# Second mixer of a two-layer decoder trunk: second pair's rotations and splits traced at high priority, compressed weights built amid the token branches, fewer scaling steps

## The chip, the cores and the metric

The kernel runs on one core of a Trainium2 chip. The metric is device time in microseconds (us), from the start to the end of one execution; 3 runs of the kernel before gave 672.49 to 674.24 us, with a median of 673.55 us. The engines that matter here are PE (matrix multiply, with transposes done as a multiply by the identity), DVE (elementwise and reductions), ACT (activations, copies out of PSUM), and SP, whose queue issues the weight loads.

## The reference, cut to what matters

A sequence of 256 tokens with 1024 features goes through two layers. Layer 0 has two attention mixers side by side, layer 1 has one mixer with three branches; behind each stands a SwiGLU FFN. The change lies in the mixer of layer 1:

```
q = rope(q).reshape(B, T, 4 groups, 4 heads, 64)
k_cmp, v_cmp = compress(rope(kc_raw), ...), compress(vc_raw, ...)   # 15 blocks of 32 tokens
p_cmp = safe_softmax(q . k_cmp * scale, block already ended)
o_cmp = p_cmp . v_cmp
o_slc = softmax(q . k_slc * scale, causal) . v_slc     # selected blocks
o_win = softmax(q . k_win * scale, causal, 512 back) . v_win
out   = g0 * o_cmp + g1 * o_slc + g2 * o_win           # g = sigmoid gates, per head
x     = x + out @ w_out
```

With 256 tokens there are 4 blocks of 64 and the 16 best are kept, so that every block is selected; the window of 512 covers all tokens. Both token branches are therefore plain causal softmaxes, over different keys and values.

## The kernel before, in words

**Precision.** A product with weights is made of three PE passes: a weight tile is split by ACT into `w_hi` (L108) and by DVE into `w_lo`, the rest (L109), activations likewise, and hi.hi, hi.lo and lo.hi are summed (`mm3`, L270 to L272). Each of the 2 x 128 tokens is a row tile, t = 0 and t = 1.

**The mixer of layer 1** (`odd_mixer`). Its 16 heads are worked in two pairs of groups, gp = 0 ("first pair") and gp = 1 ("second pair"), 8 heads each. For each pair:
- `project` makes q for both row tiles in PSUM (tile `ps_in`, 512 wide, eight 128-feature steps); `rope` on DVE rotates it (L318, L320 twice, L323) into `nq`; ACT and DVE split it into `stk` (L214, L215); PE transposes it (`pt_q`, L751) and ACT writes it out as `qS`.
- a second `project` gives the keys of both token branches (`nk`, rotated and split the same way, transposed as `pt_k`, then written by ACT as `kS` and, with its halves swapped, `kX`) and the values `vv`.
- the compressed branch, for each t: eight small matmuls into `ps_c`, and on DVE a softmax over 16 blocks for eight heads at once (L788 to L798), which ends in a transpose `pt_c` and a copy `cT`.
- the token branches, for each t and for even and odd heads (`par`): matmuls into `ps_s` (L822), then per head and branch a masked row minimum on DVE (L327) and an exponential with its sum on ACT (L328); on DVE the reciprocal of the sums (L831), their product with the gates (L832), and one scaling per head and branch (L836); then PE transposes the weights (`pt_p`, L841), ACT copies them to `pT`.
- for each t the output `ps_o`: compressed values (L849) and then token values (L857) summed in one PSUM tile; ACT and DVE split it into `aT` (L214, L215).

Then `residual` multiplies `aT` by the output weights (`ps_out`, L270 to L272), adds it to x (L308), and the next norm makes `xg` (L234) and transposes it (`pt_a`) for the FFN, whose first product is `ps_g`.

**What sets the order.** The program is traced in Python order; a scheduler in the compiler then orders each engine's instructions by priority (earlier traced first) and by when it thinks their operands and buffers are ready. Instructions passed to `pin` (`keep_in_program_order`) keep their order. Each engine runs its list strictly in order. Buffers come from pools with a fixed number of slots per tag: PSUM has 4 banks for `mm` (the projections and `ps_out`), 2 for `s` (`ps_s`, `ps_c`) and 2 for `tp` (all transposes and `ps_o`); `stk` has 2, `qS` has 3, `kS`, `kX`, `vv` and `pT` have 2, `sc` has 1 and `cT` has 2. So a later pair's transposes need the same two `tp` banks that the earlier pair's `pt_p` and `ps_o` use.

Of the kernel before, what the change touches and what calls it, by code (L numbers as in the profile page):

```python
# [10 lines left out]
AF = mybir.ActivationFunctionType  # L11
ALU = mybir.AluOpType
# [5 lines left out]
P = 128  # L18
NT = T // P
# [101 lines left out]
def trunk(tc, x, w0, w1, sm0, cw, vec, cst, out, dbg=None):  # L121
    nc = tc.nc
    V, A, G, TE = nc.vector, nc.scalar, nc.gpsimd, nc.tensor

    from contextlib import ExitStack
# [16 lines left out]
    def nat(name):  # L142
        return ap.tile([P, 512], F32, tag="nat", bufs=4, name=name)
# [25 lines left out]
    for h in range(2):  # L169
        c = slice(512 * h, 512 * h + 512)  # L170
# [18 lines left out]
    def evac(dst, src):  # L189
        A.activation(dst, src, AF.Copy)  # L190
# [83 lines left out]
    def project(aT, w):  # L274

        kk = 2
        n = KD // kk
        ps = [mm_bank("ps_in") for _ in range(NT)]
        for g in range(n):
            wh, wl = W.next()  # L280
            for i in range(kk):
                for t in range(NT):
                    mm3(ps[t][:, :w], aT[t], g * kk + i, wh[:, i], wl[:, i], g == 0 and i == 0, g == n - 1 and i == kk - 1)
        return ps
# [353 lines left out]
    def odd_mixer(nm, goff):  # L638
        aT, rs = nm.aT, nm.rs
        with tc.tile_pool(name="odd", bufs=1, reuse_waits="tile") as pool:  # L640
# [113 lines left out]
            for gp in range(2):  # L754
# [3 lines left out]
                vv = pool.tile([P, NT, 256], F32, tag="vv", bufs=2, name="vv")  # L758
                ps = project(aT, 512)
                for t in range(NT):  # L760
                    nq = nat("nq").rearrange("p (b d) -> p b d", d=64)
                    rope(pool, nq, ps[t].rearrange("p (b d) -> p b d", d=64), rs[t], t, 8, 64)
                    for h0 in (0, 4):
                        evac(qS[t][:, h0 : h0 + 4], stacked(nq[:, h0 : h0 + 4], 4, "pt_q"))
# [3 lines left out]
                for t in range(NT):  # L768
                    nk = nat("nk")[:, :256].rearrange("p (b d) -> p b d", d=64)
                    rope(pool, nk, ps[t][:, :256].rearrange("p (b d) -> p b d", d=64), rs[t], t, 4, 64)  # L770
                    A.activation(vv[:, t], ps[t][:, 256:], AF.Copy, scale=rs[t])
                    pt = stacked(nk, 4, "pt_k").rearrange("p (b r) c -> p r b c", b=2)
                    tq = slice(t * P, (t + 1) * P)
                    evac(kS[:, :, :, tq], pt)
                    for z in range(2):
                        evac(kX[64 * z : 64 * z + 64, :, :, tq], pt[64 * (1 - z) : 64 * (1 - z) + 64])


                cTs = []
                for t in range(NT):  # L780
# [22 lines left out]
                    cTs.append(cT)  # L803

                for t in range(NT):
# [5 lines left out]
                    for par in range(2):  # L811
                        pT = pool.tile([P, 2 * D], F32, tag="pT", bufs=2, name="pT")[:, : 2 * nst * 512].rearrange("p (b k j c) -> p b k j c", b=2, k=nst, j=4)
                        pTs.append(pT)
                        for j0 in range(0, 4, g):
# [14 lines left out]
                            cf = den[:, : 2 * g].rearrange("p (g b) -> p g b", b=2)  # L829
                            h0 = 2 * j0 + par  # L830
                            V.reciprocal(cf, cf)  # L831
                            V.tensor_mul(cf, cf, gates[t][:, gp, h0 : h0 + 2 * g - 1 : 2, 1:3])  # L832
                            for i in range(g):
                                for b in range(2):
                                    z = 2 * i + b
                                    V.tensor_scalar(e[:, i, b], e[:, i, b], den[:, z : z + 1], None, op0=ALU.mult)  # L836
# [11 lines left out]
                    for j in range(4):  # L848
                        mmi = TE.matmul(ob[:, j * P : (j + 1) * P], vbd[:, gp, 2 * j : 2 * j + 2].rearrange("p a d -> p (a d)"), cTs[t], start=j == 0, stop=False, skip_group_check=True)  # L849
                        if j:  # L850
                            pin(mmi)
# [152 lines left out]
```

## Time and profile before

| | |
|---|---|
| median of 3 runs | 673.55 us (672.49 to 674.24) |
| the profiled execution, its time | 673.14 us |
| its span, first to last instruction | 671.4 us |
| PE, DVE, ACT busy | 646.6, 492.2, 394.8 us |
| granted TensorE clock, mean | 0.997 |

The page's busy times are sums of instruction durations with overlaps removed. Matmuls are pipelined and their ends are modelled, so a PE that is shown busy can still be waiting a little between two starts: starts are the safer reading. The mixer of layer 1 spans about 340 to 479 us; the token branches of both pairs lie between 380 and 470 us.

### The profile page before, as it was taken

How to read it: one execution, taken by the hardware profiler on the slowest of the kernel's cores; microseconds unless marked ns; L12 is line 12 of the kernel's file. 1: busy time of each engine (PE TensorE's matmuls, PEld its weight loads, DVE VectorE, ACT ScalarE, POOL GpSimd, SP SyncE). 2: the span in 40 equal slices, each digit the busy share in tenths (PEclk: the TensorE clock that was granted, in tenths of full speed). 3: DMA queues.
4: the chain of work that ended last, by engine and by line, in shares of the span. 5: the costliest groups of instructions: out<-in, count | busy, mean ns of one | idle time of the engine just before them, and what ended most of it. 6: DMA issues, size and time to landing. Idle time of an engine off the chain costs nothing.

```text
span 671.4 us, 10018 instructions
## 1 busy us (share of the span) xinstructions
PE 646.6 (96%) x3505; PEld 537.5 (80%) x3505; DVE 492.2 (73%) x1132; ACT 394.8 (59%) x801; POOL 12.4 (2%) x24
## 2 busy tenths in 40 slices
PE   5999999999999999999999999969999999999995
PEld 4978788778888888888887877746788888888884
DVE  5999977669777787543588899696787777775424
ACT  5785748548555555433375688686675555554322
POOL 1000000000000000000000000000000000000000
PEclk9999999999999999999999999999999999999998
DMA  8844454138666666662295431400485555555601
GB/s 314 286 136 154 126 171 144 31 137 290 201 188 188 188 187 186 189 191 75 64 387 214 158 126 31 145 14 1 156 288 189 188 187 188 186 188 187 189 0 63
DMA packets 31874, 109.68 MB, mean 163 GB/s; under 512 B 3536, under 2 KB 3792, under 8 KB 31568
## 3 DMA queue, kind: packets, MB, share of 16 engines
q1 hardware_dynamic: 31392, 108.45, 49.8%
q8 instruction: 28, 0.46, 0.3%
q10 hardware_dynamic: 432, 0.59, 0.2%
q14 instruction: 22, 0.18, 0.1%
HBM read 107.98 MB, written 1.05 MB: 162 GB/s over the span
## 4 chain that ended last, share of the span: by engine, by line
PE 83%; DVE 6%; ACT 5%; DMA 3%; issue 2%; POOL 1%; SPq 0%; POOLq 0%; DVEq 0%; ACTq 0%
PE ps_g L365 12%; PE ps_u L365 12%; PE ps_out L272 7%; PE ps_out L271 7%; PE ps_out L270 7%; PE ps_u L366 6%; PE ps_g L366 6%; PE ps_in L270 4%; PE ps_in L271 4%; PE ps_in L272 4%; DMA w_raw<-in_w 3%; PE ps_o L857 2%; PE pt_p L841 2%; DVE w_lo L109 1%; ACT w_hi L108 1%
## 5 line engine op out<-in xcount | busy, mean ns | idle before, releaser
L109 DVE TENSOR_TENSOR w_lo<-w_raw,w_hi 128x1024 fp32r<-128x1024 f32 (+5 forms) x200 | 235.2, 1183 | 95.9 <-ACT w_hi L108 93.1
L108 ACT ACTIVATE w_hi<-w_raw 128x1024 fp32r<-128x1024 f32 (+5 forms) x200 | 203.2, 1023 | 142.2 <-PE ps_out L272 60.5
L365 PE MATMUL ps_g<-aW,w_hi 128*128 128x512 f32 x352 | 125.6, 399 | 0.0
L365 PE MATMUL ps_u<-aW,w_hi 128*128 128x512 f32 x352 | 125.5, 399 | 0.0
L366 PE MATMUL ps_u<-aW,w_lo 128*128 128x256 f32 x352 | 98.9, 281 | 0.0
L366 PE MATMUL ps_g<-aW,w_lo 128*128 128x256 f32 x352 | 98.9, 281 | 0.0
L365 PEld LDWEIGHTS ps_g<-aW,w_hi 128*128 128x128 f32 x352 | 66.1, 188 | 16.7 <-DVE aW L215 0.3
L365 PEld LDWEIGHTS ps_u<-aW,w_hi 128*128 128x128 f32 x352 | 66.2, 188 | 16.4
L270 PE MATMUL ps_in<-w_hi,aW 128*128 128x512 f32 (+5 forms) x208 | 77.5, 373 | 1.0 <-ACT aW L214 0.9
L272 PE MATMUL ps_in<-w_hi,aW 128*128 128x512 f32 (+5 forms) x208 | 77.0, 372 | 0.0
L271 PE MATMUL ps_in<-w_lo,aW 128*128 128x512 f32 (+5 forms) x208 | 76.6, 369 | 0.0
L272 PE MATMUL ps_out<-w_hi,hT_lo 128*128 128x512 f32 x176 | 69.4, 395 | 0.0
L271 PE MATMUL ps_out<-w_lo,hT_hi 128*128 128x512 f32 x176 | 69.1, 392 | 0.0
L270 PE MATMUL ps_out<-w_hi,hT_hi 128*128 128x512 f32 x176 | 68.4, 389 | 0.0
L366 PEld LDWEIGHTS ps_u<-aW,w_lo 128*128 128x128 f32 x352 | 66.5, 189 | 0.0
L366 PEld LDWEIGHTS ps_g<-aW,w_lo 128*128 128x128 f32 x352 | 66.5, 189 | 0.0
L270 PEld LDWEIGHTS ps_in<-w_hi,aW 128*128 128x128 f32 x208 | 39.8, 192 | 6.2 <-ACT aW L214 1.6
L328 ACT ACTIVATE e<-e,bias 128x128 f32<-128x128 f32 (+1 forms) x96 | 42.4, 446 | 3.1 <-DVE bias L327 3.1
L272 PEld LDWEIGHTS ps_in<-w_hi,aW 128*128 128x128 f32 x208 | 39.6, 191 | 4.6 <-DVE aW L215 0.5
L271 PEld LDWEIGHTS ps_in<-w_lo,aW 128*128 128x128 f32 x208 | 39.6, 191 | 4.4 <-issue 0.4
L271 PEld LDWEIGHTS ps_out<-w_lo,hT_hi 128*128 128x128 f32 x176 | 33.0, 188 | 7.6
L270 PEld LDWEIGHTS ps_out<-w_hi,hT_hi 128*128 128x128 f32 x176 | 33.0, 188 | 7.3
(215 smaller groups left out, 887.9 us busy)
## 6 DMA issues: line engine op xcount, KB each, us to landing
w_raw<-in_w SPq DMA_DIRECT2D x176, 512.0 KB, 4.3
w_raw<-in_w SPq DMA_DIRECT2D x8, 384.0 KB, 4.1
gain<-in_vec SPq DMA_DIRECT2D x4, 512.0 KB, 5.5
cw<-in_cw SPq DMA_DIRECT2D x2, 1024.0 KB, 7.4
w_raw<-in_w SPq DMA_DIRECT2D x4, 416.0 KB, 6.7
w_raw<-in_w SPq DMA_DIRECT2D x4, 328.0 KB, 6.4
w_raw<-in_w SPq DMA_DIRECT2D x4, 304.0 KB, 2.9
x<-in_x SPq DMA_DIRECT2D x4, 256.0 KB, 5.8
```

What stands on the lines that cost most here:

```text
L108: nc.scalar.activation(hi[:, :n], raw[:, :n], AF.Copy)
L109: nc.vector.tensor_sub(lo[:, :n], raw[:, :n], hi[:, :n])
L270: TE.matmul(ps, act[0][:, k], wh, start=start, stop=False)
L271: TE.matmul(ps, act[0][:, k], wl, start=False, stop=False)
L272: TE.matmul(ps, act[1][:, k], wh, start=False, stop=stop)
L328: A.activation(e, e, AF.Exp, scale=-1.0, bias=bias, accum_out=den)
L365: TE.matmul(dst[f], wh[:, i, c], wide[:, k].rearrange("p z q -> p (z q)"), start=k == 0, stop=False)
L366: TE.matmul(dst[f][:, :T], wl[:, i, c], wide[:, k, 0], start=False, stop=k == KD - 1)
L841: TE.transpose(pt[:, i, b, st], e[:, i, b, st * P : (st + 1) * P], ident)
L857: pin(TE.matmul(ob[64 * par : 64 * par + 64], vv[:, st, c : c + 64], pTs[par][:, b, st].rearrange("p j c -> p (j c)"), start=False, stop=l ...
```

## The change: what it does, and the diff

1. For the second pair only, the rotation of q and of the keys, their splits, transposes and copies are traced inside `tc.high_priority()`, which puts them ahead of everything else that is ready.
2. The compressed branch is no longer worked for t = 0 and t = 1 ahead of the token branches. `compressed(t)` is called inside the loop over t, between the even and the odd heads of that t.
3. Scaling. For t = 0 the four scalings of a group (128 columns each) become one product of 512 columns with the gated reciprocals spread out. For t = 1 the product of reciprocals and gates is dropped, and each scaling (256 columns) takes two per-row factors, the reciprocal and the gate.

```diff
+                def soon():
+                    return tc.high_priority() if gp else nullcontext()
                 ps = project(aT, 512)
-                for t in range(NT):
-                    nq = nat("nq")...
+                with soon():
+                    for t in range(NT):
+                        nq = nat("nq")...            # rope, stacked, evac as before
...
                 ps = project(aT, 512)
-                for t in range(NT):
-                    nk = nat("nk")...
+                with soon():
+                    for t in range(NT):
+                        nk = nat("nk")...            # rope, vv, stacked, evac to kS and kX as before
-                cTs = []
-                for t in range(NT):
+                def compressed(t):
                     sb = s_bank("ps_c")...
...
-                    cTs.append(cT)
+                    return cT
...
                         pTs.append(pT)
+                        if par:
+                            cT = compressed(t)
                         for j0 in range(0, 4, g):
...
-                            cf = den[:, : 2 * g].rearrange("p (g b) -> p g b", b=2)
-                            V.reciprocal(cf, cf)
-                            V.tensor_mul(cf, cf, gates[t][:, gp, h0 : h0 + 2 * g - 1 : 2, 1:3])
-                            for i in range(g):
+                            V.reciprocal(den[:, : 2 * g], den[:, : 2 * g])
+                            if t:
                                 for b in range(2):
-                                    z = 2 * i + b
-                                    V.tensor_scalar(e[:, i, b], e[:, i, b], den[:, z : z + 1], None, op0=ALU.mult)
+                                    V.tensor_scalar(e[:, 0, b], e[:, 0, b], den[:, b : b + 1], gates[t][:, gp, h0, 1 + b : 2 + b], op0=ALU.mult, op1=ALU.mult)
+                            else:
+                                cf = den.rearrange("p (g b) -> p g b", b=2)
+                                V.tensor_mul(cf, cf, gates[t][:, gp, h0 : h0 + 2 * g - 1 : 2, 1:3])
+                                V.tensor_mul(e, e, cf.unsqueeze(3).broadcast_to([P, g, 2, ns]))
```

Lines behind the diff's start are 5 to 8 higher in the changed kernel: the compressed softmax is L793 to L803 there, `ps_s` L829, the reciprocal L837, the scalings L840 (t = 1) and L843, L844 (t = 0), `pt_p` L849, `ps_o` L857 and L865.

How the lists change, at the places that the prediction speaks of. First DVE's list in the kernel before, where the first pair ends: the two last scalings, the rotation of the second pair's keys (`nk`), the split of the first pair's output (`aT`), and then the second pair's splits and the start of its compressed softmax (`sc`).

```order
L109 TENSOR_TENSOR w_lo<-w_raw,w_hi 128x1024
L836 TENSOR_SCALAR e<-e,den 128x256 x2
L318 SCALAR_TENSOR_TENSOR nk<-ps_in,rs,con 128x256
L320 SCALAR_TENSOR_TENSOR rope_b<-ps_in,rs,con 128x4x32 x2
L318 SCALAR_TENSOR_TENSOR nk<-ps_in,rs,con 128x256
L323 TENSOR_TENSOR nk<-nk,rope_b 128x256
L320 SCALAR_TENSOR_TENSOR rope_b<-ps_in,rs,con 128x4x32 x2
L109 TENSOR_TENSOR w_lo<-w_raw,w_hi 128x1024
L323 TENSOR_TENSOR nk<-nk,rope_b 128x256
L215 TENSOR_TENSOR aT<-ps_o,aT 128x512
L215 TENSOR_TENSOR stk<-nq,stk 128x4x64 x2
L788 TENSOR_TENSOR sc<-ps_c,con 128x128
```

And the same place in the changed kernel, from the scaling of the first pair's third-last group on.

```order
L837 RECIPROCAL den<-den 128x2
L109 TENSOR_TENSOR w_lo<-w_raw,w_hi 128x1024
L840 TENSOR_SCALAR e<-e,den,gates 128x256 x2
L327 ISA e,bias<-ps_s,con 128x256
...
L109 TENSOR_TENSOR w_lo<-w_raw,w_hi 128x1024 x2
L837 RECIPROCAL den<-den 128x2
L109 TENSOR_TENSOR w_lo<-w_raw,w_hi 128x1024
L840 TENSOR_SCALAR e<-e,den,gates 128x256 x2
L215 TENSOR_TENSOR stk<-nq,stk 128x4x64 x2
L215 TENSOR_TENSOR stk<-nk,stk 128x4x64
L215 TENSOR_TENSOR aT<-ps_o,aT 128x512
L215 TENSOR_TENSOR stk<-nk,stk 128x4x64
```

The rotation of the keys now stands ahead of the last two scalings of the first pair (above this piece), three of the four splits of the second pair still stand behind the last one, and no step of the compressed softmax is left between the pairs: it comes after the second pair's first eight L327.

PE's list where the first pair ends, in the kernel before: the last weights' transposes, the whole sum `ps_o`, and then the second pair's transposes amid `ps_out` and `ps_c`.

```order
L841 MATMUL pt_p<-con,e 128x128 x4
L849 MATMUL ps_o<-cT,vbd 128x128 x4
L857 MATMUL ps_o<-pT,vv 64x512 x8
L751 MATMUL pt_q<-con,stk 128x128 x4
L272 MATMUL ps_out<-w_hi,aT 128x512
```

In the changed kernel:

```order
L849 MATMUL pt_p<-con,e 128x128 x2
L857 MATMUL ps_o<-cT,vbd 128x128 x3
L865 MATMUL ps_o<-pT,vv 64x512
L751 MATMUL pt_q<-con,stk 128x128 x4
L865 MATMUL ps_o<-pT,vv 64x512 x2
L751 MATMUL pt_q<-con,stk 128x128 x4
L865 MATMUL ps_o<-pT,vv 64x512 x2
L751 MATMUL pt_q<-con,stk 128x128 x4
L865 MATMUL ps_o<-pT,vv 64x512 x3
L751 MATMUL pt_q<-con,stk 128x128 x4
L270 MATMUL ps_out<-w_hi,aT 128x512
```

The four rounds of `pt_q` moved in between the eight steps of `ps_o`.

DVE's list at the end of the second pair, in the kernel before: the last two groups, with one residual sum (L308) and one `xg` ahead of the last scaling.

```order
L836 TENSOR_SCALAR e<-e,den 128x256 x2
L308 TENSOR_TENSOR x_67<-ps_out,x_67 128x512
L831 RECIPROCAL den<-den 128x2
L234 TENSOR_TENSOR xg<-x_67,gain 128x512
L832 TENSOR_TENSOR den<-den,gates 128x2
L836 TENSOR_SCALAR e<-e,den 128x256 x2
L215 TENSOR_TENSOR aT<-ps_o,aT 128x512
```

In the changed kernel:

```order
L308 TENSOR_TENSOR x_67<-ps_out,x_67 128x512
L840 TENSOR_SCALAR e<-e,den,gates 128x256 x2
...
L234 TENSOR_TENSOR xg<-x_67,gain 128x512
L308 TENSOR_TENSOR x_67<-ps_out,x_67 128x512
L837 RECIPROCAL den<-den 128x2
L234 TENSOR_TENSOR xg<-x_67,gain 128x512
L840 TENSOR_SCALAR e<-e,den,gates 128x256 x2
L215 TENSOR_TENSOR aT<-ps_o,aT 128x512
```

Two residual sums and two `xg` now stand ahead of the last scaling, where there was one of each.

## Rows read from the trace of the kernel before

**Rows 1.** The page, part 2: PE busy in tenths, in 40 slices of 16.8 us
```profile
PE   5999999999999999999999999969999999999995
```

**Rows 2.** Busy by stage: stretch, its length, each engine's busy us (instructions), clock, DMA
```profile
380.00:400.00 20.00, 19.71 (x103) 15.54 (x103) 17.76 (x86) 16.74 (x48) 0.00 (x0) 1.00 0.35 117
400.00:421.50 21.50, 21.50 (x111) 16.04 (x110) 20.24 (x80) 17.26 (x51) 0.00 (x0) 1.00 0.20 58
421.50:435.50 14.00, 14.00 (x90) 10.07 (x89) 8.43 (x22) 8.88 (x18) 0.00 (x0) 1.00 0.38 126
435.50:465.00 29.50, 23.56 (x129) 16.91 (x127) 27.60 (x141) 25.40 (x85) 0.00 (x0) 1.00 0.04 17
465.00:479.00 14.00, 13.03 (x70) 8.46 (x68) 7.90 (x14) 5.85 (x12) 0.86 (x1) 1.00 0.01 2
```

**Rows 3.** Timeline of PE: start, us, instruction, [idle before, releaser]
```profile
450.49 0.30 PE L841 MATMUL pt_p<-con,e 128*128 128x128 f32 x1 [1.76 <-DVE e L836]
```

**Rows 4.** Timeline of DVE, from the first pair's keys to the second's minima
```profile
379.87 0.42 DVE L215 TENSOR_TENSOR stk<-nk,stk 128x256 fp32r<-128x256 f32 x1
...
420.91 0.61 DVE L836 TENSOR_SCALAR e<-e,den 128x256 f32<-128x256 f32 x2
421.43 0.48 DVE L318 SCALAR_TENSOR_TENSOR nk<-ps_in,rs,con 128x256 f32<-128x256 f32 x1
...
424.72 0.42 DVE L323 TENSOR_TENSOR nk<-nk,rope_b 128x256 f32<-128x256 f32 x1
...
435.42 0.29 DVE L327 CUSTOM_DVE_ANT_0 e<-ps_s,con 128x128 f32<-128x128 f32 x1 [1.16 <-PE ps_s L822]
```

**Rows 5.** DVE groups by form, 366 to 480 us: count, busy, mean ns, idle before
```profile
L109 DVE TENSOR_TENSOR w_lo<-w_raw,w_hi 128x1024 fp32r<-128x1024 f32 x18 | 21.9, 1222 | 0.7 <-ACT w_hi L108 0.7
L836 DVE TENSOR_SCALAR e<-e,den 128x256 f32<-128x256 f32 x32 | 9.7, 350 | 0.2
L836 DVE TENSOR_SCALAR e<-e,den 128x128 f32<-128x128 f32 x32 | 7.5, 281 | 0.0
L323 DVE TENSOR_TENSOR nq<-nq,rope_b 128x512 f32<-128x512 f32 x4 | 2.8, 691 | 0.0
L832 DVE TENSOR_TENSOR den<-den,gates 128x2 f32<-128x2 f32 x16 | 2.4, 157 | 0.2
```

**Rows 6.** DVE groups by form, whole run: factors per row and immediates
```profile
L613 DVE SCALAR_TENSOR_TENSOR pd<-e,cc 128x256 f32<-128x256 f32 x4 | 1.8, 480 | 0.0
...
L198 DVE TENSOR_SCALAR rs<-ms 128x1 f32<-128x1 f32 x8 | 1.7, 210 | 0.0
...
L194 DVE TENSOR_SCALAR r<-ms 128x1 f32<-128x1 f32 x2 | 0.3, 153 | 0.1
```

**Rows 7.** Timeline of PE between the pairs, and two `ps_out` later
```profile
421.64 0.60 PE L841 MATMUL pt_p<-con,e 128*128 128x128 f32 x4
...
423.06 3.65 PE L857 MATMUL ps_o<-pT,vv 128*64 128x512 f32 x16
426.65 0.66 PE L751 MATMUL pt_q<-con,stk 128*128 128x128 f32 x4
427.06 0.47 PE L272 MATMUL ps_out<-w_hi,aT 128*128 128x512 f32 x1
...
471.67 0.62 PE L272 MATMUL ps_out<-w_hi,aT 128*128 128x512 f32 x2
```

**Rows 8.** Timeline of ACT between the pairs
```profile
426.76 0.60 ACT L214 ACTIVATE aT<-ps_o 128x512 fp32r<-128x512 f32 x1 [2.58 <-PE ps_o L857]
...
433.51 1.20 ACT L190 ACTIVATE kX<-pt_k 64x512 fp32r<-64x512 f32 x2
```

**Rows 9.** Timeline of DVE in the second pair
```profile
447.47 0.87 DVE L836 TENSOR_SCALAR e<-e,den 128x128 f32<-128x128 f32 x4
...
462.81 0.69 DVE L308 TENSOR_TENSOR x<-ps_out,x 128x512 f32<-128x512 f32 x1
...
464.34 0.61 DVE L836 TENSOR_SCALAR e<-e,den 128x256 f32<-128x256 f32 x2
```

More of the change, by code (lines that the diff above doesn't have):

```diff
@@ L123, in trunk @@
     V, A, G, TE = nc.vector, nc.scalar, nc.gpsimd, nc.tensor
-    from contextlib import ExitStack
+    from contextlib import ExitStack, nullcontext
     ctx = ExitStack()
@@ L758, in odd_mixer @@
                 vv = pool.tile([P, NT, 256], F32, tag="vv", bufs=2, name="vv")
+                def soon():
+                    return tc.high_priority() if gp else nullcontext()
                 ps = project(aT, 512)
-                for t in range(NT):
[L761 to L764, printed above, removed]
+                with soon():
+                    for t in range(NT):
+                        nq = nat("nq").rearrange("p (b d) -> p b d", d=64)
+                        rope(pool, nq, ps[t].rearrange("p (b d) -> p b d", d=64), rs[t], t, 8, 64)
+                        for h0 in (0, 4):
+                            evac(qS[t][:, h0 : h0 + 4], stacked(nq[:, h0 : h0 + 4], 4, "pt_q"))
                 if gp == 0:
@@ L767, in odd_mixer @@
                 ps = project(aT, 512)
-                for t in range(NT):
[L769 to L776, printed above, removed]
-                cTs = []
-                for t in range(NT):
+                with soon():
+                    for t in range(NT):
+                        nk = nat("nk")[:, :256].rearrange("p (b d) -> p b d", d=64)
+                        rope(pool, nk, ps[t][:, :256].rearrange("p (b d) -> p b d", d=64), rs[t], t, 4, 64)
+                        A.activation(vv[:, t], ps[t][:, 256:], AF.Copy, scale=rs[t])
+                        pt = stacked(nk, 4, "pt_k").rearrange("p (b r) c -> p r b c", b=2)
+                        tq = slice(t * P, (t + 1) * P)
+                        evac(kS[:, :, :, tq], pt)
+                        for z in range(2):
+                            evac(kX[64 * z : 64 * z + 64, :, :, tq], pt[64 * (1 - z) : 64 * (1 - z) + 64])
+                def compressed(t):
                     sb = s_bank("ps_c")[:, :256].rearrange("p (h z n) -> p h z n", h=8, z=2)
@@ L848, in odd_mixer @@
                     for j in range(4):
-                        mmi = TE.matmul(ob[:, j * P : (j + 1) * P], vbd[:, gp, 2 * j : 2 * j + 2].rearrange("p a d -> p (a d)"), cTs[t], start=j == 0, stop=False, skip_group_check=True)
+                        mmi = TE.matmul(ob[:, j * P : (j + 1) * P], vbd[:, gp, 2 * j : 2 * j + 2].rearrange("p a d -> p (a d)"), cT, start=j == 0, stop=False, skip_group_check=True)
                         if j:
```

## The prediction

> **What bounds the kernel now.** I read the slices of the page first. PE is at 9 tenths in every slice but the first, the last and the 27th, which shows 6 [rows 1]: outside the start and the end, one stretch of the span has time to give back, and it lies in the second mixer, near 440 to 450 us. Next the busy times by stage [rows 2]. The reader is to see three different limits in them. From 380 to 421.5 us PE is busy throughout (41.2 of 41.5 us) and DVE almost so (17.76 and 20.24 us, 38.0 together): the first pair's softmaxes hide under the second pair's projections. From 421.5 to 435.5, between the pairs, PE still works all the time, on `ps_out`, while DVE is busy for 8.43 of 14 us. From 435.5 to 465 DVE is busy for 27.60 of 29.5 us and PE for only 23.56: its filler is used up, and it waits for the second pair's softmax. The longest single wait there names its releaser, 1.76 us for the scaling L836 [rows 3]. The granted clock is 1.00 in all five stretches, the higher of its two levels, so nothing is to be had or lost there.
>
> So the mixer ends when DVE's list has been worked through. DVE's own anchors [rows 4, 9] cut it into three terms: from 379.87 to the first pair's last scaling, 420.91 + 0.61 = 421.5 (stage 1); from there to the second pair's first minimum, 435.42, 13.9 us (stage 2); from there to its last scaling, 464.34 + 0.61 = 464.95, 29.5 us (stage 3). What follows, from `ps_o` over `ps_out` to the FFN, is PE's.
>
> **The change part by part.**
>
> *Scaling.* For t = 0 four scalings of 128 columns took 0.87 us [rows 9]; one product of 512 columns takes 0.69, the row of the nearest shape and kind [rows 5]. 0.18 less, in 4 groups a pair: -0.7 us. For t = 1 the small product L832 goes, 0.157 us [rows 5], in 8 groups a pair: -1.3 us. Against it stands the second factor per row. No row shows a scaling with two of them. One factor costs 0.06 at most: an instruction of one column with immediates alone takes 0.153, with one factor 0.210 [rows 6]. The second lies between nothing (both are fetched at once) and another 0.06, for 16 scalings a pair 0 to 0.9 us; a gain has no ground. I take the middle, +0.5, since neither end has a nearer row. Net -1.5 us a pair, on DVE.
>
> Here the Trainium skill speaks against the change. In "VectorE: DVE Perf Modes", section "The perf-mode tier table (the rule you actually need)", fp32 in SBUF runs at twice the rate for `tensor_scalar` and only at the single rate for `tensor_tensor`, which is what the t = 0 edit swaps in. By that alone, at the page's 0.96 GHz, an estimate of 0.27 us becomes 0.53, +0.26 in each of 8 groups, and the forecast would be 678.7 instead of 675.2. The trace decides otherwise: 128 columns take 0.281 and 256 take 0.350 [rows 5], so that most of a short scaling is a fixed part, and one long instruction beats four short ones.
>
> *Stage 1, the first pair.* The rotation of the second pair's q stood before the last scaling already. The rotation of its keys did not: 421.43 to 424.72 + 0.42 = 425.1, 3.7 us with one `w_lo` of 1.2 in it, so 2.5 us [rows 4, 5]; it now stands ahead of the first pair's last two scalings. Of the `w_lo`, one more stands ahead of the last scaling than did, 1.2 us [rows 5]. Less 1.5 of scaling: the first pair ends 2.2 us later, if DVE idles there as long as before (about 3.5 of 41.5 us). From below this is bounded by PE, which is full there: it has four more `ps_out` ahead of the last `pt_p`, which start 0.23 apart (two of them take 0.62, one alone some 0.4 [rows 7]): 0.9 us. So +0.9 to +2.2; I take +2.2, because DVE's count is the larger of two limits that both must be met. The compressed softmax only changes its place within this stage.
>
> *Stage 2, between the pairs.* Before, 13.9 us. PE did the last `pt_p` and the sum `ps_o` (421.64 to 426.65), and only then the first `pt_q` [rows 7]; the key copies followed in ACT's list at 433.51 + 1.20 = 434.7 [rows 8]. Now the `pt_q` stand inside the sum. From the last `pt_p`: 1.4 to the token part of the sum (421.64 to 423.06), 3.6 for that, four rounds of `pt_q` at 0.4 (426.65 to 427.06), 1.6 [rows 7]. PE then meets `ps_out` on the fresh `aT`, whose copy takes 0.60 [rows 8], and four of them, about 1.0; two `pt_k`, 0.8; then the copies `kS` and `kX`, 0.6 and 1.2 (the copy row of [rows 8] and its half-size neighbour), and the first `ps_s`, 0.6. Sum 11.4, with two short waits 11.7: stage 2 shortens by 2.2. Bounds: nothing, if each `pt_q` waits for its copy in the one `tp` bank that `ps_o` leaves free; and 3.5, if the waits vanish and the `aT` copy is hidden. PE loses about 1 us of cover here, in the stage where it had no gap. DVE has only five short splits left to do in these 11.7 us: the rotation, one `w_lo` and half a compressed softmax that filled its hole have gone to stages where it is full. That is the price of the edit.
>
> *Stage 3, the second pair.* DVE's 29.5 us change as follows. The first five steps of the compressed softmax of t = 0 were done in the hole and now come in line: five of 128 columns or fewer, by the row of that width 0.281 at most [rows 5], less their overlap, +1.0. One more `w_lo`, +1.2 [rows 5]. One more residual sum and `xg` ahead of the last scaling: two at 0.69, less overlap, +1.2 [rows 9]. Scaling -1.5. Sum +1.9, with DVE idle as long as before (1.9 us of 29.5). Bounds: -1.9 from there if it no longer idles at all, +2 if the compressed softmax, whose exponential now waits in ACT's list behind copies of `pT`, stops DVE once or twice more.
>
> *After it.* One `ps_out` fewer behind the last sum, -0.2; the residual work pulled ahead in stage 3 gives nothing back, since PE sets this stage (13.03 of 14 us [rows 2]). No DMA is moved on its queue past another one; at 0.04 to 0.38 of the DMA engines' time from 380 to 465 us [rows 2], a load that starts some us sooner or later meets no crowd.
>
> Sum: +2.2 - 2.2 + 1.9 - 0.2 = +1.7 us on the profiled execution, whose own time is 673.14: 674.8. The median of the runs lies 0.4 above that execution, so the forecast is 675.2 us. A measurement of this kernel can tell about 0.3%, 2.0 us, from no change; the forecast is inside it: no change that can be told, on the slow side.
>
> **The rivals.**
>
> *B, the hole really closes: 671.0.* The first pair ends when PE lets it (+0.9 instead of +2.2), and stage 3 keeps DVE busy without its 1.9 us of idling, with the second factor for nothing (-1.0 over both pairs): 675.2 - 1.3 - 1.9 - 1.0 = 671.0. For it: PE has some 6 us of idle in stage 3 [rows 2], and the first pair's sum and the second pair's transposes do now overlap. Against it: DVE's busy time sets stages 1 and 3 and falls by only 3 us in all, and the edit takes cover out of stage 2.
>
> *C, the transposes wait in turn: 677.4.* `ps_o` holds one of the two `tp` banks until its eight steps are done, so each `pt_q` needs the copy of the one before, by ACT, whose list holds the splits in between. If a round costs 0.55 more than the two steps of `ps_o` beside it cover, four cost 2.2 and stage 2 keeps its 13.9 us: 675.2 + 2.2. It decides from the point where ACT is behind PE at the first `pt_q`. Against it: two steps of `ps_o` take 0.9 us (3.65 for eight), and a copy takes 0.60 [rows 7, 8].
>
> *D, two factors cost a mode: 678.4.* A scaling with two factors per row runs like the three-operand form, 0.480 for 256 columns instead of 0.350 [rows 5, 6]: 32 at 0.13 are 4.2, less the 1.0 already counted, +3.2. Against it: the length of that form goes with its second tensor, which a scaling doesn't have.
>
> **How the numbers follow.** Forecast A 0.45, B 0.33, C 0.16, D 0.06. A's own range, from its bounds and a run's spread, is 673 to 677.3; of its 0.45, 0.32 lie within 0.3% of 673.55 (671.5 to 675.6) and 0.13 above. B gives 0.24 faster and 0.09 same; C 0.01 same and 0.15 slower; D 0.06 slower. Faster 0.24, same 0.42, slower 0.34. The range reaches below B's 671.0 and to D's 678.4: 669.5 to 678.5.
>
> **What would show it.** In the profile of the changed kernel: the first pair's last scaling 2 us later than before against the same `stk` at about 380 us, with the key rotation ahead of it (B: under 1 us); the first L327 of the second pair 11.7 us after that (C: near 14); DVE idle for most of the time between; from there to the last scaling 31 to 32 us. The scaling with two factors should read 0.35 to 0.41 (D: 0.48), the 512-column product 0.69. PE's idle time should move rather than fall: fewer gaps near 445 us, new ones between the pairs and ahead of the last `pt_p`. I am wrong in the sum if stage 3 comes out at or below 29.5, or if the key rotation at its new place fills idle time of DVE instead of adding to its work.

## The result, and the profile after

The changed kernel takes 677.71 us (median of 7 runs, 675.48 to 680.22) against 673.55 of the kernel before beside it: a ratio of 1.0074, 95% interval 1.0048 to 1.0099. A second measurement (e7 below) gave 1.0058, 1.0037 to 1.0079. It is slower by some 0.6 to 0.7%; the medians lie 4.2 and 3.1 us apart. The forecast was 675.2, no change that can be told: 677.71 lies inside its range, but the slowdown is clear of no change. (Of the profiles used below, e9's alone is of a slow execution, 684.01 us against 672.09 to 681.12 in its other runs, which alone make its ratio.)

The profiled execution took 677.44 us, with a span of 675.7 (before: 671.4). First the page: PE busy and the granted clock, in tenths, in 40 slices of 16.9 us.

```profile
PE   5999999999999999999999999888999999999995
PEclk9999999999999999999999999998999999999998
```

The one slice at 6 of [rows 1] has become three at 8 (the 26th to the 28th), and the last of them has a granted clock below 9. Then the busy times by the prediction's own stages, cut at the first split of the first pair's keys, DVE's last scaling of the first pair, the second pair's first minimum, its last scaling, and the first `ps_g`. Columns as in [rows 2].

```profile
380.65:424.55 43.90, 41.95 (x228) 33.32 (x227) 40.67 (x153) 35.84 (x100) 0.00 (x0) 1.00 0.30 97
424.55:437.43 12.88, 12.76 (x68) 7.23 (x67) 2.31 (x7) 7.25 (x15) 0.00 (x0) 1.00 0.24 80
437.43:469.02 31.59, 26.21 (x145) 19.55 (x144) 29.14 (x129) 26.41 (x86) 0.00 (x0) 0.98 0.05 17
469.02:485.60 16.58, 15.46 (x69) 9.79 (x68) 6.60 (x13) 5.74 (x12) 0.55 (x1) 0.84 0.00 1
```

| stretch | before | predicted | after | difference |
|---|---|---|---|---|
| start to 379.87 (after: 380.65) | 379.87 | 0 | 380.65 | +0.8 |
| stage 1 | 41.65 | +2.2 | 43.90 | +2.25 |
| stage 2, between the pairs | 13.90 | -2.2 | 12.88 | -1.0 |
| stage 3 | 29.53 | +1.9 | 31.59 | +2.05 |
| last scaling to the first `ps_g` | 14.08 | -0.2 | 16.58 | +2.5 |
| the FFN and the end | 192.37 | 0 | 190.1 | -2.3 |

The differences add up to the 4.3 us between the spans. Stages 1 and 3 came as forecast. Stage 2 gave less, and the stretch behind the last scaling, which the forecast had left alone, took 2.5 us more. The reason stands in PE's timeline: start, length, instruction, and in brackets the idle time before it and who ended it.

```profile
464.74 0.67 PE L849 MATMUL pt_p<-con,e 128*128 128x128 f32 x4 [0.24 <-DVE e L840]
465.80 0.67 PE L849 MATMUL pt_p<-con,e 128*128 128x128 f32 x4 [0.38 <-DVE e L840]
468.85 0.66 PE L849 MATMUL pt_p<-con,e 128*128 128x128 f32 x2 [2.38 <-DVE e L840]
...
470.15 1.49 PE L857 MATMUL ps_o<-cT,vbd 128*128 128x128 f32 x6
471.57 4.98 PE L865 MATMUL ps_o<-pT,vv 128*64 128x512 f32 x16
```

PE has nothing left to do but to wait for three scalings, the last for 2.38 us, and then the 16 products of `ps_o` take 4.98 us. In the kernel before they take 3.65 at this place, as between the pairs [rows 7]:

```profile
466.29 3.65 PE L857 MATMUL ps_o<-pT,vv 128*64 128x512 f32 x16
```

The windows of the same stretch in the changed kernel show the granted clock, the third column from the right, at its lower level (0.50 is 1.2 of 2.4 GHz) until 474:

```profile
466.00:468.00 2.00, 0.47 (x4) 0.20 (x2) 1.90 (x6) 1.59 (x6) 0.00 (x0) 0.86 0.00 0
468.00:470.00 2.00, 1.15 (x6) 1.18 (x7) 1.02 (x3) 0.00 (x0) 0.00 (x0) 0.50 0.03 8
470.00:472.00 2.00, 2.00 (x10) 1.64 (x10) 0.00 (x0) 0.60 (x1) 0.00 (x0) 0.50 0.00 0
472.00:474.00 2.00, 2.00 (x6) 0.47 (x4) 0.00 (x0) 0.00 (x0) 0.00 (x0) 0.50 0.00 0
474.00:476.00 2.00, 2.00 (x12) 0.61 (x8) 0.00 (x0) 0.00 (x0) 0.00 (x0) 0.93 0.00 0
```

Between the pairs DVE is busy for 2.31 of 12.88 us. Its timeline there reads as the prediction had it: five splits, four of them after a wait for ACT.

```profile
423.83 0.72 DVE L840 TENSOR_SCALAR e<-e,den,gates 128x256 f32<-128x256 f32 x2
428.46 0.43 DVE L215 TENSOR_TENSOR stk<-nq,stk 128x256 fp32r<-128x256 f32 x1 [3.91 <-ACT stk L214]
...
437.43 0.29 DVE L327 CUSTOM_DVE_ANT_0 e<-ps_s,con 128x128 f32<-128x128 f32 x1 [3.13 <-PE ps_s L829]
```

### The profile page after: what moved, and what is told of

Same layout as the page of the kernel before. It is cut to its first block, busy times and chain, and to the rows that moved or that the text cites. A ratio compares the mean times of both kernels' runs of the same rounds, so it can differ in the third digit from the quotient of the medians.

```text
span 675.7 us, 9983 instructions
## 1 busy us (share of the span) xinstructions
PE 648.5 (96%) x3505; PEld 540.0 (80%) x3505; DVE 489.1 (72%) x1092; ACT 396.0 (59%) x801; POOL 12.1 (2%) x24
## 4 chain that ended last, share of the span: by engine, by line
PE 84%; DVE 7%; ACT 4%; issue 2%; DMA 2%; POOL 1%; POOLq 0%; SPq 0%; DVEq 0%; ACTq 0%
PE ps_g L365 12%; PE ps_u L365 12%; PE ps_out L270 7%; PE ps_out L271 7%; PE ps_out L272 7%; PE ps_u L366 6%; PE ps_g L366 6%; PE ps_in L270 5%; PE ps_in L271 5%; PE ps_in L272 5%; ACT e L328 2%; PE ps_o L865 2%; DVE w_lo L109 2%; PE pt_a L220 1%; PE pt_p L849 1%
## 5 line engine op out<-in xcount | busy, mean ns | idle before, releaser
L109 DVE TENSOR_TENSOR w_lo<-w_raw,w_hi 128x1024 fp32r<-128x1024 f32 (+5 forms) x200 | 234.8, 1180 | 95.1 <-ACT w_hi L108 92.1
```

What stands on the lines that cost most here:

```text
L109: nc.vector.tensor_sub(lo[:, :n], raw[:, :n], hi[:, :n])
```

## The experiments

Each was timed beside the kernel before on the same chip. The stages are those of the table above; behind stage 1 stands how many weight splits `w_lo` (L109, 1.21 us each) DVE has in it, behind stage 2 DVE's busy time. "Clock" is the mean granted clock where it is not 1.00. All from the profiled execution of each kernel. (The expectations from e5 on count stage 1 from the second split of the keys, 3.8 us later: their 40.1 for the changed kernel is the table's 43.9.) The row of before is of an execution with a mean granted clock of 0.997. Of its 66 runs beside the experiments two reach this, and the others read 0.989 to 0.993, so that the row is probably shorter than in most of its executions: e6's four stretches add up to 3.0 us more than before's, at a ratio below 1.

| kernel | ratio to before (95%) | stage 1 (`w_lo`) | stage 2 (DVE) | stage 3 | behind it |
|---|---|---|---|---|---|
| before | | 41.7 (8) | 13.9 (8.3) | 29.5 | 14.1 |
| changed | 1.0074 (1.0048 to 1.0099) | 43.9 (9) | 12.9 (2.3) | 31.6, clock 0.98 | 16.6, clock 0.84 |
| e1: part 3 alone | 0.9979 (0.9951 to 1.0007) | 41.9 (8) | 13.8 (7.9) | 30.0, clock 0.89 | 14.2 |
| e2: part 2 alone | 0.9948 (0.9919 to 0.9977) | 38.4 (7) | 13.0 (9.3) | 29.9 | 14.1 |
| e3: part 1 alone | 1.0048 (1.0025 to 1.0071) | 45.5 (9) | 13.0 (3.6) | 32.5, clock 0.89 | 14.0 |
| e4: changed, PE filler | 1.0031 (1.0005 to 1.0057) | 43.9 (9) | 14.4 (2.3), clock 0.88 | 32.1, clock 0.95 | 14.2 |
| e5: parts 2 and 3 | 0.9928 (0.9902 to 0.9953) | 35.5 (4) | 13.4 (11.0) | 32.3 | 15.6, clock 0.89 |
| e6: changed, queries only | 0.9973 (0.9957 to 0.9990) | 40.3 (8) | 13.6 (5.9) | 32.8, clock 0.94 | 15.5, clock 0.90 |
| e7: changed again | 1.0058 (1.0037 to 1.0079) | 43.8 (9) | 14.5 (2.3), clock 0.88 | 31.6, clock 0.98 | 16.7, clock 0.83 |
| e8: e5, sums held back | 0.9930 (0.9905 to 0.9955) | 35.4 (4) | 13.4 (11.0) | 31.4, clock 0.99 | 17.7, clock 0.89 |
| e9: changed, DVE work in the hole | 1.0041 (1.0009 to 1.0074) | 43.9 (9) | 14.4 (7.3), clock 0.88 | 32.2, clock 0.93 | 16.8, clock 0.83 |
| e10: the same work ahead of it | 1.0116 (1.0089 to 1.0143) | 49.5 (9), clock 0.96 | 13.2 (2.4), clock 0.89 | 31.6, clock 0.99 | 15.2, clock 0.92 |
| e11: e5, PE filler | 0.9912 (0.9886 to 0.9939) | 35.4 (4) | 13.5 (11.0) | 32.2 | 14.2 |
| e12: e5, one factor | 0.9904 (0.9879 to 0.9930) | 37.7 (7) | 13.1 (9.3) | 30.2 | 14.1 |

### Each part alone: e1, e2, e3

My first theory was that parts 1 and 2 both empty the hole between the pairs and fill the stages around it.

e1, part 3 alone. Parts 1 and 2 undone:

```diff
-                    return tc.high_priority() if gp else nullcontext()
+                    return nullcontext()
...
+                cTs = [compressed(t) for t in range(NT)]
                 for t in range(NT):
...
-                        if par:
-                            cT = compressed(t)
...
```

> The kernel before with part 3 alone (one product for t = 0, two factors for t = 1). Theory O (order): parts 1 and 2 cost the time, since they take fixed DVE work out of the stretch between the pairs and set it ahead of the last scaling, and TensorE then starves and runs slower; part 3 saves what DVE's busy time shows (19.6 us of scaling, products and their sums fell to 17.3). Expected: the last scaling some 1 to 2 us earlier than before (464.95), granted clock 1.00 from 465 to 480, the time 1 to 2 us under before (672). Rival S (scaling): two factors per row stretch each scaling and the steps around it, so part 3 is itself the loss; then this kernel stands 2 to 4 us above before (676 to 678) and stage 3 is longer than 29.5 us.

Measured 0.9979, an interval that holds 1: inconclusive in time, on the side of a saving. The scaling is not the loss (rival S would have read 1.003 to 1.006).

e2, part 2 alone: part 1 undone as above, and the scaling of before put back:

```diff
-                            if t:
-                                for b in range(2):
-                                    V.tensor_scalar(e[:, 0, b], ..., op0=ALU.mult, op1=ALU.mult)
-                            else: ...
+                            V.tensor_mul(cf, cf, gates[t][...])
+                            for i in range(g):
+                                for b in range(2):
+                                    V.tensor_scalar(e[:, i, b], e[:, i, b], den[:, z : z + 1], None, op0=ALU.mult)
```

> The kernel before with part 2 alone (compressed softmax amid the token branches). Theory O: the hole between the pairs loses the first steps of the compressed softmax and gets nothing for them, stage 3 takes them in line, and two residual sums with two xg stand ahead of the last scaling instead of one: the last scaling 2 to 3 us later than before, a PE gap of over 2 us ahead of the last pt_p, granted clock below 1.00 behind it as in the changed kernel, the time 2 to 5 us above before (676 to 678). Rival H (high priority alone): part 2 is harmless, the early rotations cost the time; then this kernel is within 1 us of before and the clock stays at 1.00.

Here the theory fell: 0.9948, faster than before, and no fall of the clock in these stretches. Part 2 alone gains.

```profile
380.14:418.53 38.39, 38.33 (x212) 30.70 (x211) 35.33 (x163) 34.28 (x98) 0.00 (x0) 1.00 0.23 83
418.53:431.50 12.97, 12.94 (x75) 8.49 (x74) 9.33 (x18) 8.73 (x17) 0.00 (x0) 1.00 0.53 178
```

It has the keys' rotation still in the hole, one `w_lo` less in stage 1, and stage 1 is 3.3 us shorter. And stage 2 takes 12.97 us with DVE busy for 9.33 of them; the changed kernel, with 2.31, takes 12.88.

e3, part 1 alone: the loop over t with `compressed(t)` and the scaling as before, the high priority kept.

> The kernel before with part 1 alone (second pair's rotations and splits at high priority). Theory O: the rotation of the keys comes ahead of the first pair's last scalings (stage 1 +2 to +3 us), stage 2 gets shorter by the 1 to 2 us by which the transposes overlap, stage 3 as before (29.5): the time within 2 us of before, clock 1.00 behind the last scaling. Rival H: this part carries the loss; 4 us above before (677 to 678), and the clock falls after the last scaling.

1.0048, with an interval that holds the rival's price (4 us, 1.006). So part 1 carries a loss, but not by the rival's mechanism, since the clock does not fall behind the last scaling (it falls in stage 3); stage 1 grows by 3.8 us, more than the 2 to 3 expected.

### Taking part 1 away: e5, e6, and the changed kernel again, e7

The new theory was a floor: stage 2 lasts about 13 us whatever DVE does in it, so what part 1 moves out of it is paid in stage 1 in full. e5 is the first piece of e1's diff alone. e6 keeps the high priority for the queries and drops it for the keys:

```diff
                 ps = project(aT, 512)
-                with soon():
+                with nullcontext():
                     for t in range(NT):
                         nk = nat("nk")[:, :256].rearrange("p (b d) -> p b d", d=64)
```

> The changed kernel without part 1 (parts 2 and 3 alone). Theory F (floor): the stretch between the pairs takes about 13 us whatever DVE has to do in it (13.0 with part 2 alone, 13.1 with part 1 alone, 12.9 in the changed kernel, with DVE busy for 9.4, 3.6 and 2.4 us of it), so the rotation of the keys is free inside it and dear ahead of the first pair's last scaling. Without part 1 it goes back inside: stage 1 falls by 5 us against the changed kernel's 40.1 (to about 34.5), stage 2 stays at 13, DVE busy in it 9 to 10 us, and the time is 5 to 6 us below before's changed form and 4 to 6 us below before (ratio 0.991 to 0.995). Rival I (interaction): part 2 helps only with the old scaling, and parts 2 and 3 together come out where before does (ratio 0.998 to 1.002).

> The changed kernel with high priority for the second pair's queries alone; its keys are traced as before, and DVE's list then has their rotation behind the first pair's last scaling, while the queries' splits and transposes still stand as early as in the changed kernel. Theory F: the dear step is the rotation of the keys ahead of that scaling, so stage 1 falls to 35 to 36.5 us, stage 2 stays near 13, the ratio is 0.993 to 0.998. Rival Q (the queries' splits and transposes amid ps_o are what costs): stage 1 or 2 stays as long as in the changed kernel, the ratio 1.003 to 1.008.

> The changed kernel once more, beside the others on one chip. If the fall of the granted clock behind the last scaling belongs to its order, its trace shows it again at the same place (464 to 476 us) and the mean granted clock of its runs lies below before's. If it is a matter of one execution, the fall stands elsewhere or nowhere, and the tail from the last scaling to the first ps_g reads 14.1 us. Likewise for the FFN's pace: 391 ns per 512-column product again if it belongs to this kernel, 399 or 391 by chance if not. Time: 0.3 to 0.9% above before.

e5 measured 0.9928, as the theory has it: part 1 costs the other two parts 1.3% (1.0058 against 0.9928 on one chip), and turns a gain of 0.7% into a loss.

```profile
380.80:416.25 35.45, 35.41 (x199) 28.29 (x198) 32.15 (x140) 32.71 (x97) 0.00 (x0) 1.00 0.21 75
416.25:429.69 13.44, 13.39 (x79) 8.87 (x78) 10.96 (x19) 9.00 (x18) 0.00 (x0) 1.00 0.53 176
```

Stage 1 is 8.45 us shorter than in the changed kernel (5 were expected) and stage 2 only 0.6 longer, with DVE busy for 10.96 of its 13.44 us. What went from one to the other is read from the group of `w_lo` in stage 1, first of e5 and then of the changed kernel (count, busy, mean ns):

```profile
L109 DVE TENSOR_TENSOR w_lo<-w_raw,w_hi 128x1024 fp32r<-128x1024 f32 x4 | 4.9, 1219 | 0.0
```

```profile
L109 DVE TENSOR_TENSOR w_lo<-w_raw,w_hi 128x1024 fp32r<-128x1024 f32 x9 | 10.8, 1211 | 0.0
```

Five weight splits, 5.9 us, and the keys' rotation, 2.5 us, make up most of the 8.45. e6 separates them: its keys turn behind the last scaling again, but eight `w_lo` stand ahead of it, and stage 1 is 4.8 us longer than e5's, four `w_lo` by their rows. Its ratio, 0.9973, lies in the expected range, its stage 1 (40.3, or 36.5 as the expectation counts it) at the upper end. The queries' half of part 1 pulls weight splits ahead, the keys' half adds the rotation and one more `w_lo`, and both cost.

e7 shows which parts of the first profile belong to the kernel. Behind the last scaling the clock fell again (0.83), after the same gap:

```profile
469.67 0.66 PE L849 MATMUL pt_p<-con,e 128*128 128x128 f32 x2 [2.38 <-DVE e L840]
```

It fell in stage 2 as well, from 424 to 428, where the first profile had 1.00; there stage 2 took 14.50 us, more than before. And the FFN's pace, which had given 2.3 us back, did not come again: its products, from 500 to 612 us, first in the changed kernel's first profile and then in e7.

```profile
L365 PE MATMUL ps_u<-aW,w_hi 128*128 128x512 f32 x160 | 55.9, 391 | 0.0
```

```profile
L365 PE MATMUL ps_u<-aW,w_hi 128*128 128x512 f32 x160 | 57.0, 399 | 0.0
```

One kernel, one list, 391 ns in one execution and 399 in the other. In e3 it was the first layer's FFN that read 391. It is chance by execution, worth 2.3 us an FFN, and no part of the change's effect.

### Is DVE's work in the hole free? e9 and e10

The changed kernel with 18 additions on DVE, once behind and once ahead of the first pair's last scaling (in e10 that scaling is pinned behind them):

```diff
+                    if t and not gp:              # e9; in e10 the same ahead of the last V.tensor_scalar
+                        dm = pool.tile([P, 128], F32, tag="dm", bufs=1, name="dm")
+                        for _ in range(18):
+                            pin(V.tensor_add(dm, xs[0][:, :128], xs[0][:, :128]))
                     ob = t_bank("ps_o")
```

> The changed kernel with 18 additions of 128 columns on DVE whose result nobody reads (0.2 us apart, 3.6 us in all), placed behind the first pair's last scaling, in the stretch between the pairs; two thirds of them stand ahead of the first split stk there. Theory F (floor: PE's chain sets this stretch, DVE's work in it is free up to its idle time): stage 2 stays at 12.9 to 14.5 us, the sum of the three stages stays within 0.5 us of the changed kernel's (84.6 and 86.1), DVE's waits there fall by 3.6 us; ratio to before 1.004 to 1.008. Rival: DVE's splits are on the chain, stage 2 grows by 2.4 to 3.6 us, ratio 1.009 to 1.013.

> The changed kernel with the same 18 additions, but ahead of the first pair's last scaling. Theory F: PE has run out of other work there and waits for that scaling, so the whole 3.6 us appear: stage 1 3.2 to 3.8 us longer than the changed kernel's 40.1, stage 2 as before, ratio to before 1.010 to 1.013. Rival: stage 1 has slack, and the time is that of the changed kernel (1.006 to 1.007).

They took more than estimated, 0.32 us apart and 5.7 us in all, 5.1 of it busy, which makes the test sharper. Stages 1 and 2 of e9, and stage 1 of e10:

```profile
382.60:426.49 43.89, 41.94 (x228) 33.34 (x227) 40.66 (x154) 35.84 (x100) 0.00 (x0) 1.00 0.28 98
426.49:440.91 14.42, 14.31 (x68) 7.69 (x67) 7.28 (x24) 7.26 (x15) 0.00 (x0) 0.88 0.22 69
```

```profile
379.39:428.89 49.50, 41.93 (x227) 33.33 (x226) 45.74 (x171) 35.84 (x100) 0.00 (x0) 0.96 0.31 107
```

In the hole: DVE busy 7.28 instead of 2.31 us, stage 2 14.42, against 14.50 in e7, which has the same clock of 0.88 there. Free. Ahead of the scaling: DVE busy for 5.1 us more than in e7, and stage 1 5.7 us longer. The ratios say the same, 1.0041 (not above the changed kernel's) and 1.0116, and the rival of each is refuted. This shows the floor. That the work ahead of the scaling is paid in full is read from the profile: by the ratios 3 to 4 of the 5.7 us arrive in the time, with intervals that leave room for the rest.

### The clock behind the last scaling: e4 and e11

Nine products of 512 columns on TensorE ahead of the second pair's last `pt_p`, in e4 on the changed kernel and in e11 on e5:

```diff
+                            if gp and t and par and j0 == 3:
+                                for _ in range(9):
+                                    TE.matmul(pt.rearrange("p g b k c -> p (g b k c)"), qS[t][:, 0], kS[:, 0].rearrange("p b s -> p (b s)"), start=True, stop=True)
                             for i in range(g):
                                 for b in range(2):
                                     for st in range(nst):
                                         TE.transpose(pt[:, i, b, st], ...)
```

> The changed kernel with nine more matrix products of 512 columns, on operands that are there already, into the bank of the last pt_p, which overwrites them: TensorE works through most of its 2.4 us gap ahead of the last pt_p, and no other engine's list changes. Theory K (clock): the fall of the granted clock from 1.00 to 0.50 and 0.71 between 467 and 476 us costs 2.6 us behind the last scaling. Expected: clock 1.00 there, from the last pt_p to the first ps_g 14.2 us instead of 16.75. Since the FFN behind it ran 2.3 us shorter in the changed kernel (its 512-column products took 391 ns instead of 399), there are two forms: K1, the faster FFN follows from something else and stays, so the time is 2 to 2.6 us below the changed kernel (675); K2, the FFN's pace is given back only after a fall of the clock, so its products read 399 again and the time stays at 677 to 678. Rival N (the clock fall is not caused by the gap): the clock falls as before and the time rises by up to 0.5 us.

> Parts 2 and 3 without part 1, and nine filler products of 512 columns on TensorE ahead of the last pt_p. Theory K (the fall of the clock behind the last scaling follows TensorE's gap there): the tail from the last scaling to the first ps_g falls from e5's 15.6 us to 14.1 to 14.3, the clock reads 1.00 from 460 to 476 us, the time is 1 to 1.5 us below e5, ratio to before 0.990 to 0.992. If the fall moves to another gap, as with e4, the time is that of e5 (0.993).

In both the clock stays at 1.00 behind the last scaling, and the stretch takes 14.2 us: in e4 16.6 becomes 14.22, in e11 15.6 becomes 14.20. First that stretch in e4 and in e11, then e4's last windows ahead of it, with PE at work in the gap.

```profile
470.86:485.08 14.22, 13.13 (x67) 8.72 (x66) 6.59 (x12) 5.75 (x12) 0.55 (x1) 1.00 0.00 0
463.44:477.64 14.20, 13.11 (x67) 8.70 (x66) 6.60 (x12) 5.76 (x12) 0.55 (x1) 1.00 0.00 0
```

```profile
466.00:468.00 2.00, 1.37 (x11) 0.83 (x9) 2.00 (x9) 1.46 (x4) 0.00 (x0) 1.00 0.00 0
468.00:470.00 2.00, 2.00 (x11) 1.62 (x10) 2.00 (x6) 1.48 (x6) 0.00 (x0) 1.00 0.03 8
470.00:472.00 2.00, 2.00 (x16) 1.78 (x15) 0.86 (x3) 0.23 (x1) 0.00 (x0) 1.00 0.00 0
```

So TensorE's gap is the cause of the fall there, and the fall costs 2.4 us in the changed kernel's profile. Rival N is refuted for this place, and K2 with it: e4's second FFN reads 391 ns without a fall behind the last scaling, and so does e11's, without any fall in this mixer. In the time it shows less: 1.0031 against 1.0058 and 1.0074, 0.9912 against 0.9928, with intervals that overlap; e4's profile has falls at other places, 424 to 430 and 448 to 454.

### Two smaller questions: e8 and e12

e8 is e5 with the first residual sum held back, `mmi = V.tensor_add(xs[t][:, c], ...)` and `pin(mmi)` for t = 0, h = 0 of the second mixer.

> As e5 (parts 2 and 3), and the first residual sum of row tile 0 is held behind the split of the second pair's last output, so that two sums or products of 0.69 us stand no longer ahead of DVE's last scaling. If these stand on the path, the last scaling comes 1.2 to 2 us earlier than in e5 and the time is 1 to 2 us below e5. If the sums then delay the transposes pt_a, the stretch behind the last scaling (14.1 us) grows by as much and the time is that of e5, or up to 1 us above.

The second case: stage 3 is 0.9 us shorter and the stretch behind it 2.1 longer, the ratio the same (0.9930, 0.9928). The sums ahead of the last scaling are not worth moving by themselves.

e12 is e5 with the old scaling for t = 1:

```diff
-                            V.reciprocal(den[:, : 2 * g], den[:, : 2 * g])
+                            cf = den[:, : 2 * g].rearrange(...)
+                            V.reciprocal(cf, cf)
+                            V.tensor_mul(cf, cf, gates[t][...])
                             if t:
                                 for b in range(2):
-                                    V.tensor_scalar(..., den[:, b : b + 1], gates[...], op0=ALU.mult, op1=ALU.mult)
+                                    V.tensor_scalar(..., den[:, b : b + 1], None, op0=ALU.mult)
...
```

> As e5 (parts 2 and 3), but for t = 1 the scaling in its old form: the small product of reciprocal and gate, and one factor. By the starts in the traces two scalings with two factors hold DVE for 0.64 to 0.65 us against 0.52 to 0.53 with one, and the small product for 0.08: so the old form is 0.03 to 0.05 us shorter in each of 16 groups, 0.5 to 0.8 us in all. Theory P (part 3 saves only by the one product of t = 0): time within 1 us of e5, ratio 0.991 to 0.994. Rival (two factors save what the prediction counted, 0.157 a group): 1 to 2 us above e5, ratio 0.994 to 0.996.

0.9904, not slower than e5 (0.9928, on another chip): the two factors save nothing that shows. DVE's order moved with the edit, with seven `w_lo` in stage 1 where e5 has four, so this isn't the price of the factors alone. e12 and e11 are the fastest kernels here, both 0.9% under before; the runs don't tell them apart. Part of their gain in time, and of e2's and e5's, may be that the clock falls less often in them: the runs of e12 and e11 read a mean granted clock of 0.994 to 0.998, those of before on the same chip mostly 0.989 to 0.992, while the profiled execution of before, at 0.997, shows no fall in this mixer.

## Why the prediction was wrong, point by point

Two steps failed: the clock, put at nothing, and the gain of stage 2, put at more than twice its size. Stages 1 to 3 alone, with the clock at 0.98 to 1.00, add up to +3.3 us in the first profile where +1.9 were forecast, and 3.3 is near the 4.2 and 3.1 by which the medians differ; 1.2 of this miss of 1.4 is stage 2. (This is a sum over one profile of each kernel and no experiment of its own.)

**After it: -0.2 forecast, +2.5 between the two profiles. A step that failed.** The prediction read a granted clock of 1.00 in five stretches of one execution of before and concluded "nothing to be had or lost there". It did foresee new gaps of PE ahead of the last `pt_p`, but priced them only as waiting. e7 shows the fall again at the same place, e4 and e11 remove it with PE work alone. The gap is a price of the changed order, so the clock belonged in the sum. How much of the difference between the medians it makes, no run shows: the 13 runs of the changed kernel read a mean granted clock of 0.988 to 0.993, no lower than most of those of before (0.989 to 0.993, above). Most executions of before thus lose about as much clock, at places that no trace here shows.

**Stage 2: -2.2 forecast, -1.0 measured (clock 1.00), +0.6 in e7 (clock 0.88). The other step that failed.** A term mis-sized. The chain was right in its members but not in one length: the sum `ps_o` with its four rounds of `pt_q` was put at 5.2 us and took 7.05, from 425.83 to 432.88 (the last round at the 0.41 of [rows 7]):

```profile
425.83 1.07 PE L865 MATMUL ps_o<-pT,vv 128*64 128x512 f32 x2
426.83 0.66 PE L751 MATMUL pt_q<-con,stk 128*128 128x128 f32 x4
427.42 1.08 PE L865 MATMUL ps_o<-pT,vv 128*64 128x512 f32 x4
428.43 0.66 PE L751 MATMUL pt_q<-con,stk 128*128 128x128 f32 x4
...
430.02 0.66 PE L751 MATMUL pt_q<-con,stk 128*128 128x128 f32 x4
430.61 1.93 PE L865 MATMUL ps_o<-pT,vv 128*64 128x512 f32 x6
432.47 0.66 PE L751 MATMUL pt_q<-con,stk 128*128 128x128 f32 x4
```

That is rival C in part: between the rounds the steps of `ps_o` take 0.5 to 1.0 us each where 0.46 were counted, and the first three rounds start 1.6 us apart. ACT's timeline shows why. The second and the third round start when ACT has written their split `stk` (428.43 and 430.02), and this split stands in its list behind the copy `qS` of the round before:

```profile
427.52 0.60 ACT L190 ACTIVATE qS<-pt_q 128x512 fp32r<-128x512 f32 x1 [1.66 <-PE pt_q L751]
428.02 0.41 ACT L214 ACTIVATE stk<-nq 128x256 fp32r<-128x256 f32 x1
429.12 0.60 ACT L190 ACTIVATE qS<-pt_q 128x512 fp32r<-128x512 f32 x1 [0.70 <-PE pt_q L751]
429.61 0.41 ACT L214 ACTIVATE stk<-nq 128x256 fp32r<-128x256 f32 x1
```

And the 1.0 us are no merit of part 1: e2 and e12 have 13.0 and 13.1 without it, with the whole sum ahead of the first `pt_q`.

**Stage 1: +2.2 forecast, +2.25 measured.** Right in place and size, as a count of DVE's two lists: one more `w_lo` (nine instead of eight), the keys' rotation ahead of the last two scalings, PE waiting for them. But "the compressed softmax only changes its place within this stage" hid two large terms that nearly cancel. Parts 2 and 3 alone take 6.2 us out of stage 1 (four `w_lo` fewer), and part 1 puts 8.45 in. The prediction compared two lists; it did not ask what either part would do alone.

**Stage 3: +1.9 forecast, +2.05 measured.** Right, with one more `w_lo` (four instead of three). DVE's busy time rose by 1.46 us and its idle time by 0.6; the four terms of the prediction were not taken apart by any run.

**Scaling.** The product of 512 columns took 0.682 us (0.69 forecast), so 0.87 became 0.68. The Trainium skill's rule, in "VectorE: DVE Perf Modes", section "The perf-mode tier table (the rule you actually need)", that fp32 `tensor_tensor` runs at half the rate of `tensor_scalar`, would by the prediction's estimate have made this step a loss of 0.26. The trace doesn't agree with that estimate: it shows a gain of 0.19, since four fixed parts became one. The second factor costs 0.055 us (405 ns against 350 in [rows 5]), the upper end of the range; rival D, 0.48, is refuted. The small product L832 was counted at its full 0.157; in the trace of before the instruction behind it starts 0.07 to 0.20 us after it (460.51 to 460.58, 458.04 to 458.24), so that for t = 1 little was saved, as e12 has it.

```profile
L840 DVE TENSOR_SCALAR e<-e,den,gates 128x256 f32<-128x256 f32 x32 | 11.9, 405 | 0.0
L844 DVE TENSOR_TENSOR e<-e,den 128x512 f32<-128x512 f32 x8 | 5.4, 682 | 0.0
```

**The rivals.** B (the hole really closes, 671.0) was false as a mechanism: no order closed it below 12.9 us. The gain that it named, 0.4%, is there by the opposite road, and larger: in e5 the hole is used, not closed.

What stays open: the stretch up to stage 1 varies between 378.1 and 382.6 us over these profiles without a change in its code; what picks the FFN's pace; why the clock fell in stage 2 in e7 and not in the first profile of the same kernel; and where most executions of before lose their clock, since the one that was profiled lost none in this mixer.

## What to carry to other kernels

A hole of one engine that another engine's chain sets is a place to put work, not a thing to close: before moving work out of it, compare its length over orders with different work in it. Of a change in several parts, ask what each does alone, since a sum that fits can be two large terms that cancel. And where a change makes TensorE wait longer, add the price of the products behind the wait at the lower clock. One profile is one execution: before its stages are used as the mark for another kernel's, its mean granted clock wants comparing with those of the unprofiled runs.

## What the runs showed of the hardware

- TensorE's granted clock fell to 0.50 around the gap ahead of the second pair's last `pt_p` where it was 2.37 to 2.40 us long with shorter gaps ahead of it (the changed kernel, e5, e6, e7, e9, e10) and where it was 2.13 (e8), and not where it was 1.13 (e2) or 2.05 (e12). The length of a gap alone doesn't decide: in e1 the clock fell in stage 3 around gaps of 2.07 and 1.97 us, and in the kernel before PE idled for 2.37 us in stage 3, here, and the clock stayed at 1.00. In the changed kernel it read 0.50 from 468 to 474 us, though PE was busy again from 468.85 on.

```profile
442.93 0.30 PE L800 MATMUL pt_c<-con,sc 128*128 128x128 f32 x1 [2.37 <-DVE sc L798]
```

- The FFN's 512-column products run at 391 or at 399 ns for a whole FFN, by execution and not by kernel: 2.3 us of difference in a single profile, half of what was to be explained here.
- Eighteen additions of 128 columns that all write one tile started 0.32 us apart in e10, where 0.2 had been estimated from instructions that write different tiles.
